# Average pooling 2x2: the second-last tile's store moved behind the last loads, and the last tile cut into 16, 8, 4 and 4 units

## The chip, the cores and the metric

The kernel runs on one core of a Trainium2 chip. The metric is the device time of one execution in microseconds (us), given as the median of several runs. A run is called slow when it lies over 1.5% above the fastest of its kernel.

## The reference, cut to what matters

```python
x = np.random.randn(32, 128, 256, 256).astype(np.float32)   # kernel_size 2, stride 2
for i in range(h_out):
    for j in range(w_out):
        window = x[:, :, 2*i:2*i+2, 2*j:2*j+2]
        output[:, :, i, j] = np.mean(window, axis=(2, 3))    # output (32, 128, 128, 128) float32
```

1073.7 MB are read and 268.4 MB are written. For every four inputs there are three additions and one multiplication, so this is a kernel of transfers.

## The kernel before

A "unit" is 128 output rows: 256 KB of input, 64 KB of output, one row pair in each of 128 partitions (the first dimension of the tiles in the profile, 128x8192 for the first addition of a tile). There are 4096 units, so 128 tiles of 32 units: 8 MB in, 2 MB out. Loads are issued by SyncE (SP), stores by ScalarE (ACT). The last two tiles are cut into pieces, each with its own load and store, so that the work left after the last load is small.

```python
tail = [
    [16 * u, 8 * u, 8 * u],                          # second-last tile (u = 1 here)
    [8 * u, 8 * u, 8 * u, 4 * u, 2 * u, u, u],       # last tile
]
plan = plan[:-2] + tail
sbuf = ctx.enter_context(tc.tile_pool(name="sbuf", bufs=2))
...
for parts in plan:
    in_tile = sbuf.tile([P, G_MAIN, s * w], mybir.dt.float32, name="in_tile")
    g0 = 0
    for g in parts:
        ...
        it = in_tile[:, g0 : g0 + g]
        nc.sync.dma_start(out=it, in_=xt)
        nc.vector.tensor_add(out=it[:, :, 0:w], in0=it[:, :, 0:w], in1=...)   # the two rows
        col_sum = sbuf.tile(
            [P, G_MAIN, w_out], mybir.dt.float32, name="col_sum", bufs=3
        )
        nc.vector.tensor_add(out=col_sum[:, :g], in0=it[:, :, 0:wu:s], in1=it[:, :, 1 : wu + 1 : s])
        nc.scalar.mul(out=col_sum[:, :g], in_=col_sum[:, :g], mul=inv)
        nc.scalar.dma_start(out=ot, in_=col_sum[:, :g])
```

Every piece, even one of a single unit, takes a whole result buffer, one of three, and has to wait until the store of three pieces earlier has landed (in the trace VectorE waits so three times, 1.8 us in all; below).

## Time and profile before

| | before |
|---|---|
| median of the runs | 3106.6 us at first, 3106.4 to 3106.5 in every later series |
| span of the profiled run | 3104.8 us |
| bytes over the span | 1342.26 MB, 432 GB/s |
| VectorE, ScalarE busy | 54%, 15% |
| VectorE's waits for stores | 1.8 us in 3, all in the tail |

These are lines of the page of the kernel before. The row "DMA" is the mean busy share of the 16 DMA engines in 40 slices of the span, in tenths; "q14 instruction" counts the packets that the page puts down as instructions on queue 14, here called instruction fetches.

```profile
span 3104.8 us, 1126 instructions
DVE 1681.4 (54%) x272; ACT 465.8 (15%) x137; POOL 0.2 (0%) x4
...
DMA  9999999999999999999999999999999999999999
...
DMA packets 39176, 1342.26 MB, mean 432 GB/s; under 512 B 4352, under 2 KB 4736, under 8 KB 5888
...
q14 instruction: 8, 0.07, 0.0%
```

The transfers fill the span from end to end (nine tenths or more in all 40 slices), and no compute engine is near its limit (VectorE is busy 54%, ScalarE 15%). So only the two ends of the run are left to work on. This is the end, microsecond by microsecond, in the windows view of the kernel before. The last two columns are the mean DMA share and GB/s.

```profile
3095.00:3096.00 1.00, 0.91 (x2) 0.71 (x1) 0.00 (x0) 1.00 1.03 410
3096.00:3097.00 1.00, 0.91 (x2) 0.34 (x1) 0.00 (x0) 1.00 0.55 213
3097.00:3098.00 1.00, 0.48 (x2) 0.61 (x1) 0.00 (x0) 1.00 0.85 342
3098.00:3099.00 1.00, 0.76 (x2) 0.02 (x1) 0.00 (x0) 1.00 0.60 242
3099.00:3100.00 1.00, 0.90 (x3) 0.41 (x1) 0.00 (x0) 1.00 0.09 37
3100.00:3101.00 1.00, 0.22 (x1) 0.01 (x1) 0.00 (x0) 1.00 0.57 215
3101.00:3102.00 1.00, 0.29 (x2) 0.31 (x1) 0.00 (x0) 1.00 0.54 186
3102.00:3103.00 1.00, 0.07 (x1) 0.31 (x1) 0.00 (x0) 1.00 0.22 66
3103.00:3104.00 1.00, 0.00 (x0) 0.00 (x0) 0.00 (x0) 1.00 0.23 66
3104.00:3105.00 1.00, 0.00 (x0) 0.00 (x0) 0.00 (x0) 1.00 0.00 0
```

From 3096 us on the engines starve. The shares from there to the end at 3104.8 add up to 3.65 us, so 8.8 - 3.65 = 5.15 us of an average engine are idle.

Who waited for whom, in the waits views of the kernel before (first VectorE, then SP's own queue; in total, times, longest):

```profile
DVE col_sum L96 <- DMA out_dram<-col_sum: 1.8, 3, 0.9
...
SPq L84 <- DMA out_dram<-col_sum: 23.7, 4, 15.3
```

VectorE (DVE) waits for a result buffer in the tail, and SP waits for stores before it issues some of the last loads. The trace's records show why SP waits: eight semaphores serve all transfers in turn (544 of the 4352 landing records lie on each), and these four loads go out 0.01 to 0.02 us after the store that had used the same semaphore has landed (landed 3057.99, 3073.63, 3080.93 and 3087.04; issued 3058.01, 3073.65, 3080.95 and 3087.05).

### The profile page before, as it was taken

What the parts mean: (1) busy time and instruction counts of PE and PEld (TensorE: products, weight loads), DVE (VectorE), ACT (ScalarE), POOL (GpSimd) and SP (SyncE); (2) the same over time, 40 slices, a digit from 0 to 9 for tenths busy, and PEclk for the clock granted to TensorE, in tenths of its full rate; (3) what the DMA queues carried; (4) which work ended last, traced back from release to release, by engine and by line L of the source; (5) the groups of instructions that cost most, each with busy time, mean ns of one, the idle gap of its engine ahead of it and who ended that gap; (6) DMA issues with size and microseconds to landing.
All of it is one profiled execution on the core that took longest, in us unless ns stands there. A gap on an engine that the chain in (4) does not pass through costs nothing. (4 is left out here: it accounts for less than half of the span.)

```text
span 3104.8 us, 1126 instructions
## 1 busy us (share of the span) xinstructions
DVE 1681.4 (54%) x272; ACT 465.8 (15%) x137; POOL 0.2 (0%) x4
## 2 busy tenths in 40 slices
DVE  4555555555555555555555555555555555555556
ACT  1111111111111111111111111111111111111112
POOL 0000000000000000000000000000000000000000
DMA  9999999999999999999999999999999999999999
GB/s 418 436 439 425 436 439 425 436 438 429 433 439 430 431 439 434 427 439 435 426 438 436 427 437 436 428 436 437 427 436 437 428 436 437 429 435 437 432 431 396
DMA packets 39176, 1342.26 MB, mean 432 GB/s; under 512 B 4352, under 2 KB 4736, under 8 KB 5888
## 3 DMA queue, kind: packets, MB, share of 16 engines
q1 hardware_dynamic: 19584, 1073.75, 79.8%
q10 hardware_dynamic: 19584, 268.44, 20.2%
q14 instruction: 8, 0.07, 0.0%
HBM read 1073.74 MB, written 268.44 MB: 432 GB/s over the span
## 5 line engine op out<-in xcount | busy, mean ns | idle before, releaser
L87 DVE TENSOR_TENSOR in_tile<-in_tile 128x8192 f32<-128x8192 f32 (+4 forms) x136 | 1113.9, 8190 | 1406.7 <-DMA in_tile<-in_x_dram 1406.7
L108 ACT ACTIVATE col_sum<-col_sum 128x4096 f32<-128x4096 f32 (+4 forms) x136 | 464.5, 3415 | 2635.9 <-DVE col_sum L96 2635.9
L96 DVE TENSOR_TENSOR col_sum<-in_tile 128x4096 f32<-128x4096 f32 (+4 forms) x136 | 567.8, 4175 | 13.9 <-DMA out_dram<-col_sum 1.8
L108 ACT ACT_TABLE_LOAD x1 | 1.3, 1283 | 0.7 <-PEq L190 0.7
L190 POOL MEMSET const-bfloat16-1.0<- 128x1 bf16 x1 | 0.1, 102 | 0.0
L190 POOL MEMSET const-uint8-127<- 128x1 uint8 x1 | 0.1, 102 | 0.0
L190 POOL MEMSET const-float32-0.0<- 128x1 f32 x1 | 0.1, 99 | 0.2 <-issue 0.2
L190 POOL MEMSET const-float32-1.0<- 128x1 f32 x1 | 0.1, 99 | 0.0
## 6 DMA issues: line engine op xcount, KB each, us to landing
out_dram<-col_sum ACTq DMA_DIRECT2D x126, 2048.0 KB, 31.6
in_tile<-in_x_dram SPq DMA_DIRECT2D x5, 2048.0 KB, 27.5
in_tile<-in_x_dram SPq DMA_DIRECT2D x1, 4096.0 KB, 25.5
out_dram<-col_sum ACTq DMA_DIRECT2D x5, 512.0 KB, 12.0
in_tile<-in_x_dram SPq DMA_DIRECT2D x126, 35.1
out_dram<-col_sum ACTq DMA_DIRECT2D x1, 1024.0 KB, 12.7
in_tile<-in_x_dram SPq DMA_DIRECT2D x1, 1024.0 KB, 16.2
in_tile<-in_x_dram SPq DMA_DIRECT2D x1, 512.0 KB, 16.9
```

What stands on the lines that cost most here:

```text
L87: nc.vector.tensor_add(out=it[:, :, 0:w], in0=it[:, :, 0:w], in1=it[:, :, di * w : (di + 1) * w],)
L96: nc.vector.tensor_add(out=col_sum[:, :g], in0=it[:, :, 0:wu:s], in1=it[:, :, 1 : wu + 1 : s],)
L108: nc.scalar.mul(out=col_sum[:, :g], in_=col_sum[:, :g], mul=inv)
L190: nc = _bacc.Bacc("TRN2", target_bir_lowering=False, num_devices=1)
```

## The change

The intent: the second-last tile is not cut. Its 2 MB store is kept back and put on the load queue, behind the last loads. There it is meant not to compete with them and to give the DMA engines something to do while the last pieces are reduced. The last tile is cut into 16, 8, 4 and 4 units. There are four result buffers, and all pieces of the last tile share one of them.

```diff
-    tail = [[16*u, 8*u, 8*u], [8*u, 8*u, 8*u, 4*u, 2*u, u, u]]
+    in_pool = ctx.enter_context(tc.tile_pool(name="inp", bufs=2))
+    out_pool = ctx.enter_context(tc.tile_pool(name="outp", bufs=4))
...
+    for k in range(whole):                    # 127 whole tiles
+        it, res = tiles()
+        nc.sync.dma_start(out=it, in_=xt)
+        pool(it, res)
+        if k < whole - 1:
+            nc.scalar.dma_start(out=ot, in_=res)
+        else:
+            held = (ot, res)
+    it, res = tiles()
+    parts, a = [], 0
+    while a < rest:
+        b = rest if rest - a <= 4 else a + (rest - a) // 2
+        nc.sync.dma_start(out=it[:, a:b], in_=xt)
+        parts.append((ot, a, b))
+        a = b
+    nc.sync.dma_start(out=held[0], in_=held[1])
+    for ot, a, b in parts:
+        pool(it[:, a:b], res[:, a:b])
+        nc.scalar.dma_start(out=ot, in_=res[:, a:b])
```

(`pool` is the same two additions and one scaling as before.)

More of the change, by code (lines that the diff above doesn't have):

```diff
@@ L27, with _pool_2x2 @@
     R = n * c * h_out
-    if k == s and 2 <= k <= 4 and R > 0 and R % P == 0:
-        _nonoverlap_pool(ctx, tc, x, out, k, n, c, h, w, h_out, w_out)
+    units = R // P if R % P == 0 else 0
+    if k == 2 and s == 2 and h % 2 == 0 and w == 256 and units >= 1024:
+        _pool_2x2(ctx, tc, x, out, units)
     else:
         _generic_pool(ctx, tc, x, out, k, s, n, c, h, w, h_out, w_out)
-def _nonoverlap_pool(ctx, tc, x, out, k, n, c, h, w, h_out, w_out):
+TILE = 32
+def _pool_2x2(ctx, tc, x, out, units):
@@ L36, in _nonoverlap_pool @@
     nc = tc.nc
     P = nc.NUM_PARTITIONS
-    s = k
-    R = n * c * h_out
-    hv = h_out * s
-    xs = x if hv == h else x[:, :, 0:hv, :]
-    xv = xs.rearrange("n c (ho a) w -> (n c ho) (a w)", a=s)
-    ov = out.rearrange("n c ho wo -> (n c ho) wo")
-    assert xv.shape == (R, s * w) and ov.shape == (R, w_out)
-    wu = w_out * s
-    unit_bytes = s * w * 4
-    G_MAIN = max(1, min(R // P, (64 * 1024) // unit_bytes))
-    total_units = R // P
-    nmain, rem_units = divmod(total_units, G_MAIN)
@@ L54, in _nonoverlap_pool @@
-    plan: list[list[int]] = [[G_MAIN] for _ in range(nmain)]
-    if rem_units:
-        plan.append([rem_units])
-    if G_MAIN % 32 == 0 and nmain >= 4 and rem_units == 0:
-        u = G_MAIN // 32
-        tail = [
-            [16 * u, 8 * u, 8 * u],
-            [8 * u, 8 * u, 8 * u, 4 * u, 2 * u, u, u],
-        ]
-        assert all(sum(t) == G_MAIN for t in tail)
-        plan = plan[:-2] + tail
-    sbuf = ctx.enter_context(tc.tile_pool(name="sbuf", bufs=2))
-    inv = 1.0 / float(k * k)
@@ L71, in _nonoverlap_pool @@
-    r0 = 0
-    for parts in plan:
-        in_tile = sbuf.tile([P, G_MAIN, s * w], mybir.dt.float32, name="in_tile")
-        g0 = 0
-        for g in parts:
-            rows = P * g
-            xt = xv[r0 : r0 + rows].rearrange("(p g) f -> p g f", p=P)
-            ot = ov[r0 : r0 + rows].rearrange("(p g) f -> p g f", p=P)
-            r0 += rows
-            it = in_tile[:, g0 : g0 + g]
-            g0 += g
-            nc.sync.dma_start(out=it, in_=xt)
-            for di in range(1, k):
-                nc.vector.tensor_add(
-                    out=it[:, :, 0:w],
-                    in0=it[:, :, 0:w],
-                    in1=it[:, :, di * w : (di + 1) * w],
-                )
-            col_sum = sbuf.tile(
-                [P, G_MAIN, w_out], mybir.dt.float32, name="col_sum", bufs=3
-            )
-            nc.vector.tensor_add(
-                out=col_sum[:, :g],
-                in0=it[:, :, 0:wu:s],
-                in1=it[:, :, 1 : wu + 1 : s],
-            )
-            for dj in range(2, k):
-                nc.vector.tensor_add(
-                    out=col_sum[:, :g],
-                    in0=col_sum[:, :g],
-                    in1=it[:, :, dj : wu + dj : s],
-                )
-            nc.scalar.mul(out=col_sum[:, :g], in_=col_sum[:, :g], mul=inv)
-            nc.scalar.dma_start(out=ot, in_=col_sum[:, :g])
-        assert g0 <= G_MAIN
@@ L113, in _nonoverlap_pool, with pool @@
-    assert r0 == R, (r0, R)
+    f32 = mybir.dt.float32
+    w = x.shape[3]
+    w_out = w // 2
+    xv = x.rearrange("n c (ho a) w -> (n c ho) (a w)", a=2)
+    ov = out.rearrange("n c ho wo -> (n c ho) wo")
+    in_pool = ctx.enter_context(tc.tile_pool(name="inp", bufs=2))
+    out_pool = ctx.enter_context(tc.tile_pool(name="outp", bufs=4))
+    def pool(it, dst):
+        nc.vector.tensor_add(out=it[:, :, 0:w], in0=it[:, :, 0:w], in1=it[:, :, w:])
+        nc.vector.tensor_add(out=dst, in0=it[:, :, 0:w:2], in1=it[:, :, 1:w:2])
+        nc.scalar.mul(out=dst, in_=dst, mul=0.25)
@@ new lines, in block, with tiles @@
+    def block(r0, g):
+        rows = slice(r0, r0 + g * P)
+        xt = xv[rows].rearrange("(p g) f -> p g f", p=P)
+        return xt, ov[rows].rearrange("(p g) f -> p g f", p=P)
+    def tiles():
+        it = in_pool.tile([P, TILE, 2 * w], f32, name="in_tile")
+        return it, out_pool.tile([P, TILE, w_out], f32, name="res")
+    whole, rest = divmod(units - 1, TILE)
+    rest += 1
+    for k in range(whole):
+        xt, ot = block(k * TILE * P, TILE)
+        it, res = tiles()
[5 more added lines that the diff above has]
+            held = (ot, res)
@@ L116, in _generic_pool @@
+    it, res = tiles()
+    parts, a = [], 0
+    while a < rest:
+        b = rest if rest - a <= 4 else a + (rest - a) // 2
+        xt, ot = block((whole * TILE + a) * P, b - a)
+        nc.sync.dma_start(out=it[:, a:b], in_=xt)
[5 more added lines that the diff above has]
+        nc.scalar.dma_start(out=ot, in_=res[:, a:b])
 def _generic_pool(ctx, tc, x, out, k, s, n, c, h, w, h_out, w_out):
```

## The prediction

> **What bounds it now.** The kernel moves 1073.7 MB in and 268.4 MB out (page, HBM line). The page's DMA row is at nine tenths or more in all 40 slices, and the windows view gives a DMA share of 1.00 and 433 to 434 GB/s in every stretch from 100 to 3050 us. 1342.2 MB at 433.5 GB/s is 3096 us of a 3104.8 us span. VectorE is busy 54%, ScalarE 15%. Only about 9 us can be had at all: some 4 us before the first load's bytes flow (windows view: 0 GB/s at 3 to 4 us, 459 after), and the tail.
>
> **The tail now.** By microsecond, the windows view has the DMA share near 1 to 3096 us, then 0.55, 0.85, 0.60, 0.09, 0.57, 0.54, 0.22, 0.23, 0. Those last 8.8 us move 1.37 MB, which at 433 GB/s takes 3.2 us: about 5.6 us is lost. The chain of waits says why: the last loads were issued only at 3087.05, after a wait on a store (SP's waits on out stores: 23.7 us in 4), the last landed at 3098.8, and a serial row of one-unit pieces follows (add 0.43, add 0.29, scale 0.31, store 2.0). No other transfer is left then to fill the queues.
>
> **What the change does.** The steady state keeps its form. A fourth result buffer removes nothing there: VectorE waits for stores 1.8 us in total, all in the tail. The second-last tile is no longer split. The last tile's four loads (16, 8, 4, 4) are issued together when the tile before the second-last is reduced, and the second-last tile's 2 MB store goes behind them on the load queue. [...] it is 4.8 us of ready work (2.1 MB at 433) to keep the engines full while the last pieces are reduced. Eighteen fewer small transfers save a few tenths more.
>
> After the last load lands: adds of 4 units 1.23 + 0.69, scale 0.63, store about 2.1 us: about 4.7 us, plus perhaps 1 to 2 us of VectorE backlog from the 16-unit piece (4.42 + 2.29). Against this stand about 2 MB of held store and most of the last tile's 2 MB, up to 9 us of transfers. So the end is set by bytes, save about 1 to 2 us for the last small store's latency.
>
> **Sum (estimate).** 5.6 us lost now; about 2 us will stay; saved 3.6 us, 0.1%, all on the critical path, none in the steady state. Predicted 3103.0 us (span about 3101.3), range 3100.5 to 3106.5. Faster by over 2%: 0.01, within 2%: 0.98, slower: 0.01.
>
> **What would show it.** 433 to 434 GB/s from 100 to 3050 us unchanged; DMA share near 1 to about 3 us from the end; the last load landing 8 to 12 us before the end instead of 6; the held store issued while loads are still under way and landing in the last few us; SP's waits on stores nearly gone.
>
> **What would make it wrong.** The held store or a last store waiting for a semaphore shared with a far earlier store; the last 4-unit piece so late that VectorE, not the DMA, ends the kernel; a whole second-last tile delaying the last tile's adds; a chip whose steady rate differs by 0.1%, as much as the whole gain.

(Cut from this text, where it is marked: a sentence on how the DMA engines serve their queues, and the clause drawn from it, that the held store does not slow the last loads. Nothing in the traces showed that when it was written, so it was an assumption of the author's; e1 below tests it. No term of the sum goes with the cut: with or without it, that is 5.6 us lost less 2 us that stay, 3.6 us saved. "A few tenths more" for fewer transfers is a guess that stands in no sum; an estimate from packet times follows in the point by point.)

## The result, and the profile after

| | before | after |
|---|---|---|
| median of 4 runs | 3106.48 us | 3104.13 us |
| span of the profiled run | 3104.8 us | 3102.3 us |
| DMA packets | 39176 | 37736 |

The ratio is 0.9993, with a 95% interval of 0.9978 to 1.0007: the same within 2%. A ratio is the mean time of one kernel's fast runs over that of the other's of the same rounds, so not quite the ratio of the medians quoted. A later control on another occasion gave 3104.07 against 3106.36, so a gain of 2.3 us is repeated, though small. The prediction was 3103.0, range 3100.5 to 3106.5.

The page after:

```profile
span 3102.3 us, 1081 instructions
DVE 1679.7 (54%) x262; ACT 464.8 (15%) x132; POOL 0.2 (0%) x4
...
DMA packets 37736, 1342.26 MB, mean 433 GB/s; under 512 B 4192, under 2 KB 4192, under 8 KB 4576
...
q14 instruction: 8, 0.07, 0.0%
```

The middle of the run is what it was: the windows view shows 433 to 434 GB/s for both kernels in every stretch from 100 to 3000 us. The end after, in the same view as before:

```profile
3096.00:3097.00 1.00, 0.00 (x0) 0.42 (x1) 0.00 (x0) 1.00 1.02 422
3097.00:3098.00 1.00, 0.00 (x0) 0.00 (x0) 0.00 (x0) 1.00 0.98 385
3098.00:3099.00 1.00, 0.00 (x0) 0.00 (x0) 0.00 (x0) 1.00 0.66 258
3099.00:3100.00 1.00, 0.00 (x0) 0.00 (x0) 0.00 (x0) 1.00 0.19 76
3100.00:3101.00 1.00, 0.00 (x0) 0.00 (x0) 0.00 (x0) 1.00 0.08 31
3101.00:3102.00 1.00, 0.00 (x0) 0.00 (x0) 0.00 (x0) 1.00 0.00 0
```

The engines are full to 3098 us instead of 3096, and then the share does not stop: it fades out over three microseconds. The shares from 3097 us to the end at 3102.3 add up to 1.91, so 5.3 - 1.91 = 3.4 us of an average engine are still idle. The prediction had 2. The waits, in the two views as before; VectorE's waits for stores are no longer in its list, and of SP's these are left:

```profile
SPq L91 <- ACT res L56: 16.7, 1, 16.7
...
SPq L91 <- DMA out_dram<-res: 9.4, 1, 9.4
```

Line 91 is the held store. It waits until its tile is scaled, and no load waits for a store any more.

Why does the share fade out instead of stopping? The page gives a mean over 16 engines, and the waits views count a transfer as landed when its last engine is done (for the last load before, the last of its records and the landing in the chain view are both at 3098.78 us). The trace has sixteen landing records for each transfer (4192 for the 262 transfers after the change), read here as one from each of the 16 DMA engines, and they do not come at the same time. The next table is worked out from these records (it is not a view of the profile). For the last five transfers of each kernel it gives the time at which the last of the 16 engines was done, counted back from the last landing of the run, and in brackets the spread from the first engine to the last.

```
before   -3.33 (1.84)   -2.33 (0.21)   -1.98 (0.19)   -1.01 (0.16)   0.00 (0.17)
after    -2.48 (2.56)   -1.26 (2.56)   -0.63 (2.56)    0.00 (2.56)     (and -3.70 (3.78) ahead of these)

the 16 engines in the last landing after, us from the first:
0.00 0.02 0.03 0.04 0.05 0.06 0.08 0.12 0.18 0.19 0.28 0.29 0.39 1.65 1.90 2.56
```

The records do not name the engines. Thirteen are done within 0.4 us of each other; three come 1.65, 1.90 and 2.56 us after the first. The last lies 2.07 us behind the mean. In the kernel before the spread closes to 0.2 us in the last four stores: the slow engines had caught up, by this reading because all were waiting for the next small piece (the DMA share there is 0.09 to 0.57). In the changed kernel it stays at 2.56 us to the very end: the slowest engine seems never to be without work. Its last three landings fit that: they are 1.22, 0.63 and 0.63 us apart, about what eight packets, a sixteenth of the 128 of each store, take in the trace (8 x 159 ns and 8 x 84 ns). So here the critical path is read as one DMA engine; by that reading the idle time of the other fifteen costs nothing. e13 and e5_pool_1024 below test that.

The spread is also not there from the start. In the changed kernel it is 0.4 us at 67 us and grows in steps. The trace has eight instruction fetches on queue 14 during the run, each a packet of 8 KB that takes 309 ns, and the steps sit right behind them (again worked out from the records, for the landings of loads):

```
fetches at (us)        spread of the landings, before -> after them
525.3 and 540.4        0.42 -> 0.82 -> 1.04
918.2                  (the largest spread does not grow)
1541.4 and 1556.9      1.10 -> 1.37 -> 1.87
2466.8                 1.73 -> 1.88
2581.8 and 2597.5      1.89 -> 1.92 -> 2.71
```

The spread is a rough gauge. Between the fetches it drifts by up to 0.2 us (down to 0.87 by 1000 us, up to 1.10 by 1518 us), and other runs show spread that no fetch made: in e13 the loads' spread is 2.44 us at 68 us, before any fetch, and the stores' 4.8 us at 3021 us, with the time of the changed kernel; in e12 the loads' spread is 4.17 us at 3022 us and 2.07 in the tail. What sets the engines apart there is open. So a spread taken somewhere in a run is not by itself a loss at its end.

This gave the theory that the experiments test.

### The profile page after: what moved, and what is told of

It reads as the page before. It is cut to its first block, busy times and chain, and to the rows that moved or that the text cites. A ratio compares the mean times of both kernels' runs of the same rounds, so it can differ in the third digit from the quotient of the medians.

```text
span 3102.3 us, 1081 instructions
## 1 busy us (share of the span) xinstructions
DVE 1679.7 (54%) x262; ACT 464.8 (15%) x132; POOL 0.2 (0%) x4
## 2 busy tenths in 40 slices
DMA packets 37736, 1342.26 MB, mean 433 GB/s; under 512 B 4192, under 2 KB 4192, under 8 KB 4576
## 4 chain that ended last, share of the span: by engine, by line
DMA 72%; DVE 27%; issue 0%; DVEq 0%; ACT 0%; SPq 0%
DMA in_tile<-in_x_dram 72%; DVE in_tile L54 18%; DVE res L55 9%; DVEq L55 0%; ACT res L56 0%; SPq L74 0%
## 5 line engine op out<-in xcount | busy, mean ns | idle before, releaser
L54 DVE TENSOR_TENSOR in_tile<-in_tile 128x8192 f32<-128x8192 f32 (+1 forms) x131 | 1113.0, 8496 | 1404.2 <-DMA in_tile<-in_x_dram 1404.2
L56 ACT ACTIVATE res<-res 128x4096 f32<-128x4096 f32 (+1 forms) x131 | 463.5, 3538 | 2630.9 <-DVE res L55 2630.9
L55 DVE TENSOR_TENSOR res<-in_tile 128x4096 f32<-128x4096 f32 (+1 forms) x131 | 567.0, 4328 | 11.8 <-DVE in_tile L54 0.5
```

The lines of the kernel that those rows point to most:

```text
L55: nc.vector.tensor_add(out=dst, in0=it[:, :, 0:w:2], in1=it[:, :, 1:w:2])
L56: nc.scalar.mul(out=dst, in_=dst, mul=0.25)
```

## The experiments

Theory: the changed kernel is at the limit of its slowest DMA engine, which instruction fetches have put behind. What the tail of the kernel before lost was the time in which that engine starved, and holding the store is one of several ways to end that. Rivals: the held store is the gain; the new cut of the last tile is the gain; the adds, scaling and store of the last piece set the end. Twelve kernels ran. All gave correct results except one.

| run | second-last tile | its store | last tile | result buffer | median, us | against before, us |
|---|---|---|---|---|---|---|
| before | 16, 8, 8 | at once | 8 8 8 4 2 1 1 | one each piece | 3106.4 | |
| e8_before_whole | whole | at once | 8 8 8 4 2 1 1 | one each piece | 3107.64 | +1.2 |
| e10_before_one_result | 16, 8, 8 | at once | 8 8 8 4 2 1 1 | shared | 3105.29 | -1.2 |
| e9_no_hold_old_split | whole | not held | 8 8 8 4 2 1 1 | shared | 3104.48 | -2.0 |
| e1_no_hold | whole | at once | 16 8 4 4 | shared | 3104.60 | -1.8 |
| e2_hold_old_split | whole | held | 8 8 8 4 2 1 1 | shared | 3104.45 | -2.0 |
| c_after (the change) | whole | held | 16 8 4 4 | shared | 3104.07 | -2.3 |
| e3_hold_no_split | whole | held | 32 | shared | 3117.0 | +10.6 |

### e1_no_hold: the change without the held store

```diff
-        if k < whole - 1:
-            nc.scalar.dma_start(out=ot, in_=res)
-        else:
-            held = (ot, res)
+        nc.scalar.dma_start(out=ot, in_=res)
...
-    nc.sync.dma_start(out=held[0], in_=held[1])
```

> The changed kernel, but the second-last tile's store goes out on the ACT queue at once, like all others; the split 16, 8, 4, 4 stays. Theory (the held store is the gain: it lets the last loads land early and is work left over for the end): the gain goes, about 3106 us (3105.5 to 3107), and the last load lands within 6 us of the last store's landing. Rival (the gain is the fewer and larger pieces of the tail): stays at 3104.1, within 0.5.

Measured: 3104.60 us (3104.43 to 3104.71). My expectation, and the prediction's main argument with it, fell: without the held store the kernel loses only 0.5 us of its 2.3. What the prediction assumed of the loads (the clause that is cut there) fits the runs: with the store held the last load lands 5.6 us earlier. The timeline of e1 at the last piece (start and length in us, engine, line, operation; in brackets how long the engine was idle before, and what ended that):

```profile
3084.29 0.34 ACTq L76 DMA_DIRECT2D out_dram<-res  x1
...
3097.22 1.22 DVE L54 TENSOR_TENSOR in_tile<-in_tile 128x1024 f32<-128x1024 f32 x1 [3.15 <-DMA in_tile<-in_x_dram]
...
3099.27 0.94 ACTq L90 DMA_DIRECT2D out_dram<-res  x2
```

The second-last tile's store goes out at 3084.29, the last load competes with it and lands only at 3097.2 (in the changed kernel at 3091.6), and the last stores are issued at 3099.3 to 3100.2. But the slowest engine still had stores of the earlier pieces to move: the stores that landed 2.95 and 1.73 us before the end have a spread of 2.6 us, as in the changed kernel, and only the last two have 0.2. So that engine seems to have run dry only just before the end.

### e2_hold_old_split: the change with the old cut of the last tile

```diff
-    while a < rest:
-        b = rest if rest - a <= 4 else a + (rest - a) // 2
+    for g in (8, 8, 8, 4, 2, 1, 1):
+        b = a + g
```

> The changed kernel with the last tile split 8, 8, 8, 4, 2, 1, 1 as before, the store still held on the load queue. Theory (the held store is the gain, and the end is set by bytes and by the slowest DMA engine, not by the last piece's work): 3103.5 to 3104.5, the same as the change. Rival (the split 16, 8, 4, 4 is the gain): about 3106. If the last piece's latency were what ends the changed kernel, the one-unit pieces would gain 0.5 to 1 us: 3103.3.

Measured: 3104.45 us (3104.26 to 3104.99). As the theory expected; the new cut is worth some 0.4 us beside a held store. That is about what its packets cost. The new cut has three loads and three stores fewer, 144 packets each (1440 fewer for the ten transfers fewer, from the two pages). The packet times in the trace are 84 ns for 2 KB, 159 ns for 4 KB and 2418 ns for 64 KB: from 2 to 4 KB they rise by 75 ns, which leaves an estimated 9 ns that do not go with the bytes; 864 packets over 16 engines at 9 ns are an estimated 0.5 us. The pieces of one unit gained nothing, so the latency of the last piece is not what ends the kernel (e13 tests that directly).

### e3_hold_no_split: the last tile not cut at all

```diff
     while a < rest:
-        b = rest if rest - a <= 4 else a + (rest - a) // 2
+        b = rest
```

> The changed kernel with the last tile not split at all, the store held. Theory: the held store is only 4.8 us of work, and an unsplit last tile leaves 8.7 + 4.4 + 3.6 us of adds and scale and 4.8 us of store plus latency after its load, so the DMA engines idle some 10 us: 3114 to 3118 us. If holding alone were enough, 3104.

Measured: 3117.0 us (3116.95 to 3117.16), as the theory expected. Holding is no substitute for cutting: 2 MB of store cover about 5 us (2.1 MB at the measured 433 GB/s are 4.8), and an uncut tile needs 17 us of adds and scaling after its load (8.69 + 4.43 + 3.62 in the timeline).

### e8_before_whole: the kernel before with its second-last tile whole

```diff
     tail = [
-            [16 * u, 8 * u, 8 * u],
+            [32 * u],
```

> The kernel before with one edit: its second-last tile is not split (its store goes out at once on ACT as one 2 MB store). Theory (only the held store counts): like before, 3105.5 to 3107. Rival (fewer small transfers in the second-last tile give part of the gain): 3105 or less.

Measured: 3107.64 us (3107.6 to 3107.71), 1.2 us slower than before. Neither expectation had that. VectorE's waits for stores doubled. The waits view of e8:

```profile
DVE col_sum L96 <- DMA out_dram<-col_sum: 3.6, 3, 2.2
```

The third piece of the last tile now waits for the whole 2 MB store ahead of it (landed at 3096.71), because its result buffer is one of three in rotation, and the pieces behind it are late too. The waits view understates this, as it counts only the time in which VectorE had nothing else to do. The second addition of the third piece in e8, and in e9 below, where the pieces share one buffer:

```profile
3096.83 1.93 DVE L96 TENSOR_TENSOR col_sum<-in_tile 128x1024 f32<-128x1024 f32 x2 [0.88 <-DMA out_dram<-col_sum]
...
3090.58 1.23 DVE L55 TENSOR_TENSOR res<-in_tile 128x1024 f32<-128x1024 f32 x1
```

It comes 6.3 us later in e8. This pointed at the result buffers.

### e10_before_one_result: the kernel before with one result buffer for each tile

```diff
+        col_tile = sbuf.tile(
+            [P, G_MAIN, w_out], mybir.dt.float32, name="col_sum", bufs=3
+        )
         g0 = 0
         for g in parts:
...
-            col_sum = sbuf.tile(
-                [P, G_MAIN, w_out], mybir.dt.float32, name="col_sum", bufs=3
-            )
+            col_sum = col_tile[:, g0 - g : g0]
```

> The kernel before with one edit: one result buffer for each input tile, shared by its pieces, instead of a new one for each piece. Theory: the three waits of VectorE for stores (1.8 us) go, and the end comes 1 to 2 us earlier: 3104.5 to 3105.5. Rival (those waits are off the chain, or the held store was needed): 3106.4, within 0.4.

Measured: 3105.29 us (3105.19 to 3105.43), inside the theory's range. This edit holds no store and keeps every cut, and it gives half of the gain. The three waits of VectorE for stores are gone.

### e9_no_hold_old_split: both named parts of the change undone

The diffs of e1 and e2 together.

> The changed kernel with both named parts undone: the store not held, the last tile split 8, 8, 8, 4, 2, 1, 1. What is left of the change is that the second-last tile is whole and that all pieces of a tile share one result buffer (the kernel before takes a new one of three for each piece, so a piece waits until the store three pieces earlier has landed). Theory (the waits for result buffers cost the kernel before its time; holding and splitting are two ways around the same wait for the slowest DMA engine): near 3105, 1 us or more below before with its second-last tile whole (3107.6). Rival (without the held store a fine split costs time in itself): 3106.5 to 3107.6.

Measured: 3104.48 us (3104.27 to 3104.54), 3.2 us below e8, from which it differs in the shared result buffer and in the pools (their number and the count of result buffers). So without either of the parts that give the change its name, 2.0 of 2.3 us are there. Of these, 0.8 us come on top of e10: with the second-last tile whole, the tail has fewer transfers, fewer loads wait for the semaphore of a store, and the last load is issued 10 us earlier (first e10, then e9):

```profile
L87 SPq DMA_DIRECT2D in_tile<-in_x_dram x2: 328/380/432, 3087.0 to 3087.4; - x2
...
L85 SPq DMA_DIRECT2D in_tile<-in_x_dram x1: 328/328/328, 3077.2 to 3077.2; - x1
```

It lands at 3095.5 instead of 3099.2 us. The whole tile thus costs 1.2 us where each piece takes its own buffer (e8) and gains 0.8 where the pieces share one. In e2 and e9 the second-last tile's store is issued at nearly the same time, 3087.2 and 3087.4 us (3 us later than in e1, after the first piece's scaling), once on the load queue and once on the store queue, so the pair compares just that: 0.03 us. The reason that it makes no difference: in e9 the last load lands at 3095.5 us, 7.3 us before the end of the span, and the last landings are spread over 1.7 to 2.6 us. By these landings the slowest engine was busy to within about a microsecond of the last one in both. A caveat: since ACT's order of instructions differs, e1 and e9 are not the same "not held" with another cut.

### e13_late_piece: the last piece delayed

```diff
     for ot, a, b in parts:
+        if b == rest:
+            nc.vector.tensor_add(out=scr, in0=it[:, a:b, 0:w], in1=it[:, a:b, w:])
         pool(it[:, a:b], res[:, a:b])
```

> The changed kernel with one useless addition of 1.22 us (into a scratch tile) on VectorE ahead of the last 4-unit piece, so that the last store is issued about 1.2 us later, at about 3097.7 instead of 3096.45 us. Theory (the slowest DMA engine still has stores to move and ends the kernel): time as the change, 3104.0 to 3104.4, and the last landing still spread over more than 1.5 us. Rival (the chain of adds, scale and store of the last piece ends it): 3105.2 to 3105.4.

Measured: 3104.15 us (3104.13 to 3104.32, 5 runs), against 3104.07 to 3104.13 for the change. The useless addition and the late store stand in the timeline of e13:

```profile
3093.44 1.22 DVE L96 TENSOR_TENSOR scr<-in_tile 128x1024 f32<-128x1024 f32 x1
...
3097.33 0.34 ACTq L98 DMA_DIRECT2D out_dram<-res  x1
```

and of the changed kernel the last store in its timeline:

```profile
3096.45 0.34 ACTq L94 DMA_DIRECT2D out_dram<-res  x1
```

The last store is issued 0.9 us later, and it costs less than 0.1 us. The work of the last piece is off the critical path, with at least 0.8 us of slack. The spread of the last landing is 2.42 us.

### e5_pool_1024 and e5_pool_2048: more instruction fetches

```diff
+    scr = ctx.enter_context(tc.tile_pool(name="scr", bufs=1)).tile([P, 8], f32, name="scr")
+    for _ in range(1024):                     # or 2048
+        nc.gpsimd.memset(scr, 0.0)
```

> The changed kernel with 1024 tiny memsets on the idle GpSimd, which touch nothing else: 8 more instruction fetches of 64 KB. Theory (the end is set by the slowest DMA engine, which instruction fetches have put behind): the spread over the 16 DMA engines of a landing grows from 2.56 us. The present spread came from 8 fetches, [...] some 0.3 to 0.85 us each; 8 more on one engine are 2.5 to 6.8 us, so the spread ends at 2.6 to 7 us and the time at 3104 to 3108.5, rising by what the spread rises. Rival (spread is something else, and fetches do not add up): spread 2.6, time 3104.1.

(The "64 KB" in this text means all eight fetches together; one is 8 KB. "0.3 to 0.85 us each" is an estimate; the trace has 309 ns for a fetch packet, and 2.56 us of spread over three fetches would be 0.85. That all eight more go to one engine was an assumption.)

> The same with 2048 memsets, 16 more fetches. Theory: the spread ends at 5 to 13.6 us, twice what 1024 memsets put on that engine, and the time at 3106.5 to 3115, each microsecond of spread above 2.6 adding a microsecond to the time. Rival: spread 2.6, time 3104.1.

Measured with 1024: 3107.28 us (3107.16 to 3107.34), 3.2 us more than the change. The page of this kernel shows the eight additional fetches and nothing else that changed in the transfers:

```profile
DMA packets 37744, 1342.33 MB, mean 432 GB/s; under 512 B 4192, under 2 KB 4192, under 8 KB 4576
...
q14 instruction: 16, 0.13, 0.0%
```

The fetches come at 13 to 159 us. By 169 us the spread of the loads is 6.25 us, and it is still 6.11 us at 2974 us: one engine is that far behind the first, the next one 2 to 3 us. In this run the engine that was put behind stayed behind. At that time the spread is 3.53 us above that of the changed kernel (6.11 against 2.58), and the last landing comes 3.2 us later. (In the last landing itself the spread is only 3.08 us, as the other engines there wait for the last stores.) GpSimd's memsets were done after 166 us and nothing waits for them. A rival is that the memsets and not the fetches put the engine behind. The steps speak against it: the memsets run evenly, but from 69 us on the spread rises by 0.64 to 0.67 us from one load to the next where one fetch lies between (at 74.4, 136.8 and 158.6 us), and by 1.29 us where two do (at 96.2 and 115.0 us). So it is the fetches that cost 3 us at the far end of the run. After the first of these fetches the spread is 1.22 us, after the other seven 6.25 us: 0.72 us for each on average, more than twice the 309 ns that the packet itself has in the trace.

Measured with 2048: a median of 3156.66 us, with runs from 3130.15 to 3243.5; the slowest, which is also the profiled one, counts as slow. The theory's range was 3106.5 to 3115, so it was missed on the far side. The profile can therefore only be described: in it the spread passes 11 us at 320 us and stays near 12 until 2620 us, and in that time the rate in the windows view is 407 to 413 GB/s, where the other kernels have 433. By 2843 us the spread has fallen to 8.6 us, and the rate is back at 430 GB/s and above:

```profile
1000.00:1500.00 500.00, 252.76 (x39) 71.12 (x20) 0.00 (x0) 1.00 1.00 410
...
2900.00:3000.00 100.00, 55.47 (x10) 14.46 (x4) 0.00 (x0) 1.00 1.01 432
```

Packets of 64 KB took up to 2855 ns at the ninetieth percentile instead of 2418. In the changed kernel a load is issued about 13 us after the landing of the tile two before it (3043.0 and 3056.3 us) and a tile takes 24.2 us (additions start at 3018.9 and 3043.0), so by this estimate the fastest engines can be at most some 11 us ahead before they run out of work; that fits where the trouble starts and ends. Why the packets themselves become slower then, and why the runs differ so much, no run here shows, and it stays open.

### e11_fewer_instr: fewer instruction fetches (wrong result on purpose)

```diff
-        nc.vector.tensor_add(out=it[:, :, 0:w], in0=it[:, :, 0:w], in1=it[:, :, w:])
         nc.vector.tensor_add(out=dst, in0=it[:, :, 0:w:2], in1=it[:, :, 1:w:2])
-        nc.scalar.mul(out=dst, in_=dst, mul=0.25)
```

> Wrong result on purpose: the changed kernel without its row addition and without its scaling, so with half of the instructions on VectorE and ScalarE and the same transfers. Theory (the end is set by the DMA engine that instruction fetches have put behind): fetches during the run fall from 8 to 4 or 5, the last spread from 2.56 to 0.8 to 1.8 us, and the time falls by what the spread falls, 0.8 to 1.8 us, to 3102.3 to 3103.4. Rival (the work of the last pieces ends the kernel): those pieces lose 1.9 us each of adds and scaling, and the time falls by 1 to 2 us with a spread that stays; the landings tell the two apart.

Measured: 3103.82 us (3103.73 to 3104.06). Half of the instructions on VectorE (566.9 us busy instead of 1679.7) and all on ScalarE are gone, and the time falls by 0.25 us. The fetches fell only from 8 to 6 and the last spread from 2.60 to 2.04 us. Direction right, size missed: I overrated how many fetches would go, and of the 0.55 us of spread only half came back in time. As a second result this run shows how far the kernel is from any limit of its compute engines.

### e12_tile40: a version meant to beat both

Tiles of 40 units (101 of them, then 28 held and 28 cut into 14, 7, 3 and 4), two result buffers.

```diff
-TILE = 32
+TILE = 40
...
+    sizes = [TILE] * 101 + [28]
```

> A correct version meant to beat both: the changed kernel with tiles of 40 units instead of 32 (101 of them, then 28 held and 28 split 14, 7, 3, 4; two result buffers), so a fifth fewer instructions. Theory: 5 or 6 fetches during the run instead of 8, spread 1.7 to 2.1 us instead of 2.56, time 3103.2 to 3103.8. Rival (larger tiles cost a longer start and a longer tail): 3104.5 or more.

Measured: 3108.38 us (3108.23 to 3108.51), so it failed. The page counts 7 fetches, where I had expected 5 or 6; the last landing's spread did fall, to 2.00 us. But a load of 80 KB for each partition goes out as two packets of 40 KB (the page of e12 has 28336 packets on the load queue, 101 x (256 + 16) + 6 x 144):

```profile
DMA packets 43463, 1342.25 MB, mean 432 GB/s; under 512 B 3392, under 2 KB 3520, under 8 KB 4032
...
q14 instruction: 7, 0.06, 0.0%
```

That is 5727 packets more than the change has, 358 for each engine; at 9 ns an estimated 3.2 us, which is more than the spread gave back. About 1.6 us of the loss is not explained (4.3 measured + 0.5 from the spread - 3.2). No correct version that I tried beats the change.

### c_after: control

> The changed kernel itself once more, as control on the same chip as the other runs of this call: 3104.1 us, spread of the last landings over the DMA engines 2.56 us.

Measured: 3104.07 us (3103.98 to 3104.17) and a spread of 2.60 us.

## Why the prediction was right or wrong, point by point

- **Right: what bounds the kernel.** The steady state is bound by DMA and the change leaves it alone: 433 to 434 GB/s at a DMA share of 1.00 before and after, and with VectorE busy 18% instead of 54% and ScalarE not at all the time falls by 0.25 us (e11). The time, 3104.13, is inside the range, and "within 2%" held. That is weak support for the rest: the range reaches to 3106.5, the time of the unchanged kernel, and the saving was 2.35 us where 3.6 was predicted. As far as the saving was counted on the held store, the hit was luck, as the fourth point shows.
- **Right: the end is set by bytes, not by the last piece's latency.** The sentence was "So the end is set by bytes, save about 1 to 2 us for the last small store's latency." e13 delayed the last store by 0.9 us for less than 0.1 us. (The bytes that count are those of the slowest DMA engine, which the prediction did not have.)
- **The mis-sized term: "5.6 us lost now; about 2 us will stay; saved 3.6 us".** 3.4 us stayed, not 2, and mostly not for the latency of the last store. The 5.6 us is a loss of the average engine, by bytes. After the change 2.07 us of what stays is the distance from the mean engine to the slowest one, which by the landings is not idle; 0.94 us lies between the last landing and the end of the span (0.81 before). In shares of an average engine, 5.15 us idle became 3.4, so 1.75 us. Ten transfers fewer are 1440 packets fewer, 90 for each engine, at 9 ns an estimated 0.8 us. Together 2.55, and the span fell by 2.5. The prediction read a mean where a maximum was wanted.
- **Wrong: where the gain comes from.** "It is 4.8 us of ready work ... to keep the engines full while the last pieces are reduced" was meant as the gain. The held store is worth 0.5 us with the new cut (e1) and 0.03 us with the old one (e2 against e9). Undoing both named parts leaves 2.0 of 2.3 us.
- **Overlooked: the waits in "A fourth result buffer removes nothing there: VectorE waits for stores 1.8 us in total, all in the tail."** As it stands the sentence is right, for it speaks of the steady state, and no run tests a fourth buffer alone. But the 1.8 us in the tail were read and then left out of the sum. The whole gain to be had was small, and half of it lay there. The edit that only lets the pieces of a tile share a result buffer, with three buffers as before, gave 1.2 us (e10), and I had not seen that the rewrite made it.
- **Wrong in a count: "Eighteen fewer small transfers."** There are ten fewer (272 before, 262 after); the packets of these are the estimated 0.8 us above.
- **The signs.** The last load landed at 3091.6 us, 10.7 us before the end: predicted 8 to 12. The held store was issued at 3084.1 us while loads were still under way. SP's waits on stores went from 23.7 to 9.4 us, of which none is a load's. The DMA share is near 1 to 4.3 us from the end, predicted about 3.

What is shown: that the last piece has slack (e13), that more fetches lengthen the run and put one engine further behind (e5_pool_1024), that shared result buffers give half of the gain (e10), and that with the second-last tile whole as well 2.0 of the 2.3 us are there (e9, in which the pools and a fourth buffer come along and were not tested apart). What is argued from these and not shown by a run of its own: that the remaining 1.2 us between e10 and the change are about 0.8 us of packets and the last loads landing early enough to leave stores for the slowest engine; and that it is fetches that made the whole 2.56 us of spread in the changed kernel (e11 removed two of the eight and got 0.25 us).

## What to carry to other kernels

Here the mean DMA share at the end overstated what could be won: of the 3.4 us that it left idle after the change, 2.07 were the distance from the mean engine to the slowest. So look at how far the 16 landings of one transfer lie apart (2.56 us here): by that reading the slowest engine ended this kernel, and a last store issued 0.9 us later cost under 0.1 us (e13). Before adding a scheme that fills a tail with held work, look whether small pieces wait for result buffers in rotation (1.8 us here), and whether loads wait for the semaphores of stores (23.7 us here); letting the pieces of a tile share one buffer was the cheaper half of the gain here (1.2 of 2.3 us, e10). Read the whole diff, not only its description: undoing the two parts that gave this change its name left most of its gain in place.
